# A bidirectional trunk of two layers on Trainium2: scan products that alternate array halves, and dense operands at one place

## The chip, the cores and the metric

One core of one Trainium2 chip runs the whole kernel. Its engines are TensorE (PE, matrix products, with its weight loads PEld), VectorE (DVE), ScalarE (ACT), GpSimd (POOL) and SyncE (SP, which issues transfers). The metric is the device time of one execution in microseconds, less being better.

## The reference

Two layers over 2048 tokens of width 1024, in single precision. The even layer projects the input once; the columns feed a gated DeltaNet (4 heads of 128) and an RWKV-7 time mixing (8 heads of 64), each run forward and backward over the tokens and summed. The odd layer is a Hyena operator with long filters by FFT. After each: an output projection, a LayerNorm, and a gated embedding. What the change touches most is the RWKV-7 recurrence:

```
def step(state, xs):
    r_t, w_t, k_t, v_t, a_t, b_t = xs
    sa = einsum('bhvk,bhk->bhv', state, a_t)
    state = state * w_t[:, :, None, :] + sa[..., None] * b_t[:, :, None, :] + v_t[..., None] * k_t[:, :, None, :]
    return state, einsum('bhvk,bhk->bhv', state, r_t)
...
wkv = rwkv7_scan(r, w_f, k, v, a_vec, b_vec) + flip_t(rwkv7_scan(flip_t(r), flip_t(w_b), ...))
...
h = layer_norm(DEEPNORM_ALPHA * h + mix @ w_out[i], ln_g[i], ln_b[i])
e = rms_norm(p[i] @ ple_w[i], ple_norm[i])
h = h + sigmoid(h @ ple_gate[i]) * e
```

## The kernel before, in words

Seven stages follow one another: the even layer's projection (`phase_a`, 0 to 929 us of the profiled execution), the scans (`scans`, 929 to 2114), a tail (`tail`, output projection, norm and gate, 2114 to 2520), the odd layer's projection (`phase_d`, 2520 to 3330), the Hyena convolutions (3330 to 4120) and the second tail (4120 to 4578).

The dense products (projections and tails) split each single-precision operand into a high and a low part of a faster format and add three products, high with high, low with high and high with low, each 128x128 by 512 columns (for some 80). The moving operands are xh and xl in `phase_a`, hh and hl in `phase_d`; the weights there are wh and wl. In a tail the weights are wo (output projection, in pool tl_o), wg (gate, 8 pairs of tiles in pool tl_w) and we (embedding, 2 pairs, tl_w), printed as tg<-wo0h,yh and so on. Pools place tiles one behind the other in a partition, so the size of one tile sets where the later ones start.

The scans work in chunks of 64 tokens, 32 chunks a direction, first forward, then backward. DeltaNet and RWKV-7 run side by side. RWKV-7 has three parts for a chunk. `rk_front` builds from decay, r, k, a and b the operands X, bk and LY (X and LY have four buffers, `ahead` is 4); for two chunks at once it first forms the decay from w2 and tw (64 rows each, at the upper or lower half of the partitions by direction). Its products ga and gb take the two halves of the rows, four pairs of heads each. An `inverter` then forms the inverse E of a triangular matrix in half precision. `rk_chain` is the recurrence: z from X and the state rS, u from E and z, the new state from bkT and rU, and the outputs y from X with rS and from LY with rU. Products of the recurrence write 64 columns of outputs at one half of the array (a matrix of 64 in its columns: shape 128*64), those of ga and gb use half of its rows (64*128), those of y with X use a quarter (64*64). The chunk's y lies on 64 partitions; ScalarE copies it (forward) or DVE adds it (backward) into Y. `rk_front` for chunk i waits until chunk i − 4 is through the chain (`st["n"]`).

Nothing of the scans is issued as it is written. The class `Ahead` records all engine operations (a call at line 162 runs or records one), and `flush` plans them for all engines at once: `graph` gives each a cost, `forward` walks in time and takes for each free engine the ready operation of the highest priority, `backward` forms new priorities from the plan, up to eleven plans are made, and the shortest by these costs is issued, all at line 638. So all rows of the scans carry L638, and tiles of SBUF are printed as grain.N (pieces of 8 KB that several tiles share) and PSUM tiles as bank. Operations that write one PSUM tile share the highest priority among them (`together`). For PE `forward` prefers, among operations whose priority is within 3.0 us of the best, one of the same `kind` as the last; the kind is a boolean, `slow`: a single-precision product at the lower half of the outputs with over 64 stationary columns.

Of the kernel before, what the change touches and what calls it, by code (L numbers as in the profile page):

```python
# [20 lines left out]
P = 128  # L21
# [122 lines left out]
class Ahead:  # L144
# [101 lines left out]
    class Banks:  # L246
# [7 lines left out]
        def tile(self, shape, dt, name=None, tag=None, bufs=1):  # L254
# [5 lines left out]
            m.bank[name] = base + len(ring) % bufs  # L260
            ring.append(name)
            return m.view(self.t[0][:shape[0], :math.prod(shape[1:])], shape, name)

    def __init__(self, tc):
# [3 lines left out]
        self.plan, self.bank, self.before, self.count, self.exact = None, {}, {}, 0, False  # L268
# [127 lines left out]
    def graph(self, ops):  # L396
# [38 lines left out]
        for i, (e, (w, r)) in enumerate(zip(g["eng"], rw)):  # L435
            if e == "P":
                m = math.prod(r[0].shape[1:])
                g["load"][i] = m / (2400 if ops[i][1] == "transpose" else 1200) if r[-1].dtype == F32 and not self.beside(w[0]) else 0.0
                g["move"][i] = math.prod(w[0].shape[1:]) / (1200 if r[-1].dtype == F32 else 2400)
        g["outer"] = {y: set().union(*(deps[i] for i in users[y])) - users[y] for y in users if y in self.bank}  # L440
# [37 lines left out]
    def together(self, prio):  # L478

        top = {}  # L480
        for y, p in zip(self.g["gen"], prio):
            if y:
                top[y] = max(top.get(y, 0.0), p)
        return [top[y] if y else p for y, p in zip(self.g["gen"], prio)]

    def forward(self, deps, prio, bank=None):
# [16 lines left out]
        order, tick, seen, warm, kind, kept = [], 0, 0.0, False, False, 0.0  # L503
        slow, load, move = g["slow"], g["load"], g["move"]
        while len(order) < n:
# [50 lines left out]
            if e == "P":  # L556
# [5 lines left out]
                seen += cols[i]  # L562
                c = (c + max(0.0, load[i] - kept)) * (1 if warm else 2)
# [37 lines left out]
    def flush(self, stay):  # L601


        self.stay = stay
# [39 lines left out]
class Trunk:  # L644
# [121 lines left out]
    def phase_a(self, src):  # L766
# [3 lines left out]
        with ExitStack() as ctx:  # L770
# [9 lines left out]
            sab = wp.tile([16, 3], F32, name="abs", tag="abs", bufs=1)  # L780
# [465 lines left out]
    @staticmethod  # L1246
    def stages():

        return {"f": {}, "i": {}, "n": 0}
# [160 lines left out]
    def rk_setup(self, d):  # L1410
# [3 lines left out]
        R["w2"] = cp.tile([P, 512], F32, name="rk_w2s")  # L1414
        nc.sync.dma_start(R["w2"][64 * di:64 * di + 64], A["rk_w2"][0, di])
# [12 lines left out]
    def rk_front(self, d, wp, ps, I, st):  # L1428
# [7 lines left out]
        dr = slice(64 * di, 64 * di + 64)  # L1436
        bank = lambda: ps.tile([P, 4, P], F32, name=self.n("pp"), tag="prep", bufs=4)
# [3 lines left out]
        for n, t in enumerate(order(NT)):  # L1441
# [3 lines left out]
            nc.sync.dma_start(tw[dr], self.s_wd[dr, t * P:(t + 1) * P])  # L1445
            while 2 * n >= st["n"] + I["ahead"]:
                yield None
            yield tw,
            p_ = bank()
            for p in range(4):  # L1450
                nc.tensor.matmul(p_[:, p, :], R["w2"][dr, p * P:(p + 1) * P], tw[dr], start=True, stop=True)
# [15 lines left out]
            for j, c in enumerate(order(2)):  # L1467
                i = 2 * n + j
                while i >= st["n"] + I["ahead"]:
# [10 lines left out]
                ga, gb = bank(), bank()  # L1480
                for p in range(4):
                    nc.tensor.matmul(ga[:, p, :], bk[lo, p].rearrange("p q t -> p (q t)"), X[lo, p, 0:2, :], start=True, stop=True)
                for p in range(4):
# [20 lines left out]
    def rk_chain(self, d, wp, ps, st, done, gone):  # L1504
# [4 lines left out]
        bank = lambda: ps.tile([P, 4, 64], F32, name=self.n("ch"), tag="ch", bufs=4)  # L1509
# [752 lines left out]
```

## Time and profile before

| what | value |
|---|---|
| runs, us | 4584.09, 4582.79, 4581.69; median 4582.79 |
| profiled execution, us | 4579.95, its span 4578.0 |
| PE busy, us | 4403.1 (96%) |
| PE weight loads, us | 3674.2 (80%) |
| DVE busy, us | 2798.2 (61%) |
| ACT busy, us | 2325.1 (51%) |
| POOL busy, us | 1741.6 (38%) |
| mean granted clock of PE | 0.982 |

An engine's busy time is the union of its instructions' records. Records of products overlap, since the next starts before the last is drained; what one product costs PE is read from the distance between starts. A single-precision product of the scans leaves two records, others one.

### The profile page before, as it was taken

Reading aid. Unit: us, or ns where it says so; the run is one execution under the profiler, and the core shown is the slowest. Engines: PE = TensorE matmul, PEld = TensorE weight load, DVE = VectorE, ACT = ScalarE, POOL = GpSimd, SP = SyncE. Lnnn points to the kernel's source line nnn. Section 1 sums busy time; section 2 is a strip of 40 time slices with the busy share of each in tenths; the row PEclk is TensorE's granted clock in tenths of the full one; section 3 lists DMA queues with packets and bytes.
Section 4 is the critical chain, followed back from the end, with each engine's and each line's share of the span. In section 5 each row is a group of like instructions: output and inputs, shape, how many; then the busy total and the mean of one; then the engine's idle time right before and its main releaser. Section 6 shows DMA issues by size and latency. Waiting matters only on the chain. (4 is left out here: it accounts for less than half of the span.)

```text
span 4578.0 us, 86860 instructions
## 1 busy us (share of the span) xinstructions
PE 4403.1 (96%) x34638; PEld 3674.2 (80%) x34638; DVE 2798.2 (61%) x4535; ACT 2325.1 (51%) x4533; POOL 1741.6 (38%) x1609
## 2 busy tenths in 40 slices
PE   8999999989999999997999999999989999997999
PEld 6777777778888888885888777777879999986887
DVE  5455555577777788886444334444368888875443
ACT  5334333367667666664222323333279998973222
POOL 0121220244554667764333100000068787763332
PEclk9999999989999999998999999999999999998999
DMA  3233323343333334434211311111131111104211
GB/s 117 71 84 88 86 74 83 88 138 97 105 97 109 120 121 140 139 104 165 68 65 59 102 66 64 64 53 64 51 104 42 50 60 33 48 29 173 71 65 43
DMA packets 379293, 388.95 MB, mean 85 GB/s; under 512 B 111706, under 2 KB 298817, under 8 KB 370441
## 3 DMA queue, kind: packets, MB, share of 16 engines
q1 hardware_dynamic: 378889, 383.40, 26.7%
q8 instruction: 274, 4.49, 0.4%
q14 instruction: 130, 1.06, 0.1%
HBM read 263.18 MB, written 120.13 MB: 84 GB/s over the span
## 5 line engine op out<-in xcount | busy, mean ns | idle before, releaser
L162 ACT COPY pb<-g 128x512 f32<-128x512 f32 (+1 forms) x264 | 154.9, 587 | 900.2 <-PE g L162 900.0
L162 PE MATMUL g<-xh,wh 128*128 128x512 f32 (+1 forms) x1088 | 439.8, 404 | 0.1
L162 PE MATMUL g<-xh,wl 128*128 128x512 f32 (+1 forms) x1088 | 435.1, 400 | 0.0
L162 PE MATMUL g<-xl,wh 128*128 128x512 f32 (+1 forms) x1088 | 434.3, 400 | 0.0
L162 PE MATMUL g<-hh,wh 128*128 128x512 f32 x1024 | 411.2, 402 | 0.5 <-ACT hh L162 0.4
L162 PE MATMUL g<-hl,wh 128*128 128x512 f32 x1024 | 404.3, 395 | 0.0
L162 PE MATMUL g<-hh,wl 128*128 128x512 f32 x1024 | 402.2, 393 | 0.0
L162 DVE SCALAR_TENSOR_TENSOR cv<-pb,pc,cv 128x512 f32<-128x512 f32 (+1 forms) x304 | 225.7, 749 | 181.9 <-ACT pb L162 95.8
L638 POOL MEMSET grain.4123_32497<- 64x2048 f32 x1 | 1.8, 1801 | 756.5 <-PE g L162 756.5
L162 PEld LDWEIGHTS g<-xh,wh 128*128 128x128 f32 (+1 forms) x1088 | 206.3, 190 | 52.8 <-issue 3.7
L162 PEld LDWEIGHTS g<-xl,wh 128*128 128x128 f32 (+1 forms) x1088 | 205.7, 189 | 50.8 <-DVE xl L162 0.4
L162 PEld LDWEIGHTS g<-xh,wl 128*128 128x128 f32 (+1 forms) x1088 | 206.1, 189 | 49.1 <-issue 0.7
L162 POOL TENSOR_TENSOR sq<-tm 128x512 f32<-128x512 f32 x48 | 51.9, 1092 | 481.2 <-ACT tm L162 481.2
L162 PEld LDWEIGHTS g<-hh,wh 128*128 128x128 f32 x1024 | 192.3, 188 | 50.3 <-ACT pb L162 3.2
L162 PEld LDWEIGHTS g<-hl,wh 128*128 128x128 f32 x1024 | 192.3, 188 | 48.9
L162 PEld LDWEIGHTS g<-hh,wl 128*128 128x128 f32 x1024 | 192.3, 188 | 47.5 <-issue 1.9
L162 ACT CAST h<-sp 128x512 fp32r<-128x512 f32 (+1 forms) x96 | 46.2, 513 | 336.5 <-PE sp L162 336.5
L162 DVE SCALAR_TENSOR_TENSOR u<-u,tg 128x512 f32<-128x512 f32 x64 | 44.0, 687 | 239.8 <-PE tg L162 239.8
L162 POOL TENSOR_TENSOR yl<-y,yh 128x1024 fp32r<-128x1024 f32 x32 | 78.1, 2440 | 283.8 <-ACT yh L162 283.8
L162 DVE SCALAR_TENSOR_TENSOR pm<-pb,hcol,a 128x512 f32<-128x512 f32 x64 | 73.2, 1155 | 148.6 <-ACT pb L162 148.1
L162 DVE SCALAR_TENSOR_TENSOR a<-pb,hcol,a 128x512 f32<-128x512 f32 x128 | 94.4, 741 | 104.7 <-ACT pb L162 65.5
L162 ACT ACTIVATE tg<-tg 128x512 f32<-128x512 f32 x64 | 37.2, 582 | 214.7 <-PE tg L162 214.7
(733 smaller groups left out, 13286.9 us busy)
## 6 DMA issues: line engine op xcount, KB each, us to landing
grain.45_7042<-s_rk SPq DMA_DIRECT2D x32, 1024.0 KB
wr<-in_even_w_in SPq DMA_DIRECT2D x33, 512.0 KB
y<-s_y SPq DMA_DIRECT2D x32, 512.0 KB
wr<-in_odd_w_in SPq DMA_DIRECT2D x32, 512.0 KB
xr<-in_x SPq DMA_DIRECT2D x32, 256.0 KB
s_qk<-cm SPq DMA_DIRECT2D x32, 256.0 KB
s_kv<-tm SPq DMA_DIRECT2D x32, 256.0 KB
s_gate<-th SPq DMA_DIRECT2D x32, 256.0 KB
```

Of the source, the lines that this page charges most:

```text
L162: f(*a, **kw)
L638: r = f(*map(bare, a), **{k: bare(x) for k, x in kw.items()})
```

## The change

Two things change. The first is in the scans. `flush` gets a flag that only the scans set: a product's kind is then which of the four array shapes it uses, a change of kind costs 0.095 in the plan, a product on a part of the array costs half as much as before unless it sits in the same place as the one before it, and weight loads cost nothing. Two PSUM tiles can be twins that share a priority. ga and gb are twins and are written alternately. The outputs y of two chunks are formed together when the second is through, in twin tiles, with products that alternate over the array, and are copied or added on 128 partitions; rS and rU get a third buffer for that, and `rk_front` waits for a count `st["m"]` that rises by two when a pair's y is written. w2 is filled up with zeros to 128 rows, and tw is loaded with all 128 rows. The second is in the dense stages: a tile is widened and two unused ones are put in front, so that later tiles start elsewhere. In bytes mod 512 of a partition, moving and stationary operand go from 224 and 256 to 224 and 224 in `phase_a`, from 64 and 224 to 224 and 224 in `phase_d`, from 160 and 224 to 224 and 224 for wg, and from 160 and 32 to 224 and 32 for we; for wo they are 224 and 224 before and after.

```diff
@@ -251,13 +251,15 @@
-        def tile(self, shape, dt, name=None, tag=None, bufs=1):
+        def tile(self, shape, dt, name=None, tag=None, bufs=1, twin=None):
...
             m.bank[name] = base + len(ring) % bufs
+            m.twin[name] = m.twin[twin.name] if twin is not None else name
             ring.append(name)
@@ -265,7 +267,7 @@
-        self.plan, self.bank, self.before, self.count, self.exact = None, {}, {}, 0, False
+        self.plan, self.bank, self.twin, self.before, self.count, self.exact = None, {}, {}, {}, 0, False
@@ -437,6 +439,18 @@
+        g["part"], g["spot"] = [None] * len(ops), [0] * len(ops)
+        if self.parts:
+            for i, (e, (w, r)) in enumerate(zip(g["eng"], rw)):
+                if e == "P":
+                    k, m = r[0].shape[0], math.prod(r[0].shape[1:])
+                    g["part"][i] = (k > 64, m > 64)
+                    where = lambda x: x.offset // x.ap[0][0] % P >= 64
+                    g["spot"][i] = where(w[0]) + 2 * where(r[0])
+                    if g["part"][i] != (True, True) and r[-1].dtype == F32:
+                        g["cost"][i] = 0.004 + max(math.prod(w[0].shape[1:]), 52) / 1200, g["cost"][i][1]
+                    g["load"][i], g["slow"][i] = 0.0, g["part"][i]
         g["outer"] = {y: set().union(*(deps[i] for i in users[y])) - users[y] for y in users if y in self.bank}
@@ -478,10 +492,11 @@
         top = {}
-        for y, p in zip(self.g["gen"], prio):
+        gen = [y and self.twin[y] for y in self.g["gen"]]
+        for y, p in zip(gen, prio):
             if y:
                 top[y] = max(top.get(y, 0.0), p)
-        return [top[y] if y else p for y, p in zip(self.g["gen"], prio)]
+        return [top[y] if y else p for y, p in zip(gen, prio)]
@@ -500,7 +515,7 @@
         got, spare, rows = {}, [(0.0, k) for k in range(8)], []
-        order, tick, seen, warm, kind, kept = [], 0, 0.0, False, False, 0.0
+        order, tick, seen, warm, kind, kept, spot, parts = [], 0, 0.0, False, False, 0.0, 0, self.parts
@@ -560,6 +575,13 @@
                 seen += cols[i]
+                if parts:
+                    if kind != slow[i]:
+                        c += 0.095
+                    elif slow[i] != (True, True) and spot == g["spot"][i]:
+                        c *= 2
+                    spot = g["spot"][i]
                 c = (c + max(0.0, load[i] - kept)) * (1 if warm else 2)
@@ -598,10 +620,11 @@
-    def flush(self, stay):
-        self.stay = stay
+    def flush(self, stay, parts=False):
+        self.stay, self.parts = stay, parts
         ops, self.plan, self.exact = self.plan, None, True
@@ -777,7 +800,7 @@
             rk = wp.tile([P, T], F32, name="rk", tag="rk", bufs=1)
-            sab = wp.tile([16, 3], F32, name="abs", tag="abs", bufs=1)
+            sab = wp.tile([16, 128], F32, name="abs", tag="abs", bufs=1)[:, 0:3]
@@ -1246,7 +1269,7 @@
-        return {"f": {}, "i": {}, "n": 0}
+        return {"f": {}, "i": {}, "n": 0, "m": 0}
@@ -1412,6 +1435,7 @@
         R["w2"] = cp.tile([P, 512], F32, name="rk_w2s")
+        nc.gpsimd.memset(R["w2"][64 - 64 * di:P - 64 * di], 0.0)
         nc.sync.dma_start(R["w2"][64 * di:64 * di + 64], A["rk_w2"][0, di])
@@ -1433,8 +1457,7 @@
         lo, hi, al = slice(0, 64), slice(64, 128), slice(0, P)
-        dr = slice(64 * di, 64 * di + 64)
-        bank = lambda: ps.tile([P, 4, P], F32, name=self.n("pp"), tag="prep", bufs=4)
+        bank = lambda twin=None: ps.tile([P, 4, P], F32, name=self.n("pp"), tag="prep", bufs=4, twin=twin)
@@ -1442,13 +1465,13 @@
             tw = sb("tw", [P], 2)
-            nc.sync.dma_start(tw[dr], self.s_wd[dr, t * P:(t + 1) * P])
-            while 2 * n >= st["n"] + I["ahead"]:
+            nc.sync.dma_start(tw, self.s_wd[:, t * P:(t + 1) * P])
+            while 2 * n >= st["m"] + I["ahead"]:
                 yield None
...
             for p in range(4):
-                nc.tensor.matmul(p_[:, p, :], R["w2"][dr, p * P:(p + 1) * P], tw[dr], start=True, stop=True)
+                nc.tensor.matmul(p_[:, p, :], R["w2"][:, p * P:(p + 1) * P], tw, start=True, stop=True)
             G = sb("G", [4, P], 1)
@@ -1466,7 +1489,7 @@
                 i = 2 * n + j
-                while i >= st["n"] + I["ahead"]:
+                while i >= st["m"] + I["ahead"]:
                     yield None
@@ -1477,10 +1500,10 @@
                 yield bk, X
-                ga, gb = bank(), bank()
+                ga = bank()
+                gb = bank(ga)
                 for p in range(4):
                     nc.tensor.matmul(ga[:, p, :], bk[lo, p].rearrange("p q t -> p (q t)"), X[lo, p, 0:2, :], start=True, stop=True)
-                for p in range(4):
                     nc.tensor.matmul(gb[:, p, :], bk[hi, p].rearrange("p q t -> p (q t)"), X[hi, p, 1:3, :], start=True, stop=True)
@@ -1506,7 +1529,7 @@
         NC = 2 * NT
-        bank = lambda: ps.tile([P, 4, 64], F32, name=self.n("ch"), tag="ch", bufs=4)
+        bank = lambda twin=None: ps.tile([P, 4, 64], F32, name=self.n("ch"), tag="ch", bufs=4, twin=twin)
@@ -1514,7 +1537,7 @@
             for nm in ("rS", "rU"):
-                x = sb(nm, [4, 2, 64], 2)
+                x = sb(nm, [4, 2, 64], 3)
                 v = self.s_rv[tok(i):tok(i) + 64].rearrange("t s (a c) -> t s a c", a=4)
@@ -1524,7 +1547,7 @@
         nc.vector.memset(rS[hi, :, 1, :], 0.0)
-        Y = None
+        Y, two = None, []
         for i in range(NC):
@@ -1538,7 +1561,7 @@
             t, c, X, LY, E, bkT, pcl = (u[k] for k in ("t", "c", "X", "LY", "E", "bkT", "pcl"))
-            hp = slice(64 * c, 64 * c + 64)
+            two.append((slice(64 * c, 64 * c + 64), X, LY, rS, rU))
             if i + 1 < NC:
@@ -1566,23 +1589,31 @@
                 nc.vector.tensor_tensor(nS[hi, :, 1, :], pd[hi], sp[hi], op=ALU.add)
-            py = [bank(), bank()]
-            for p in range(4):
-                for q, r in ((0, lo), (1, hi)):
-                    nc.tensor.matmul(py[q][hp, p, :], X[r, p, 1, :], rS[r, p, q, :], start=(p == 0), stop=False)
-            for p in range(4):
+            if i % 2:
+                py = [bank()]
+                py.append(bank(py[0]))
+                for p in range(4):
+                    for k in range(2):
+                        for j, (hp, X, _, S_, _) in enumerate(two):
+                            q = k ^ j
+                            r = (lo, hi)[q]
+                            nc.tensor.matmul(py[q][hp, p, :], X[r, p, 1, :], S_[r, p, q, :], start=(p == 0), stop=False)
+                for p in range(4):
+                    for q in range(2):
+                        for hp, _, LY, _, U_ in two:
+                            nc.tensor.matmul(py[q][hp, p, :], LY[:, p, q, :], U_[:, p, q, :], start=False, stop=(p == 3))
                 for q in range(2):
-                    nc.tensor.matmul(py[q][hp, p, :], LY[:, p, q, :], rU[:, p, q, :], start=False, stop=(p == 3))
-            for q in range(2):
-                if late:
-                    nc.vector.tensor_tensor(Y[hp, :, q, :], py[q][hp], Y[hp, :, q, :], op=ALU.add)
-                else:
-                    nc.scalar.copy(Y[hp, :, q, :], py[q][hp])
-            if i % 2:
+                    if late:
+                        nc.vector.tensor_tensor(Y[:, :, q, :], py[q], Y[:, :, q, :], op=ALU.add)
+                    else:
+                        nc.scalar.copy(Y[:, :, q, :], py[q])
+                two = []
                 if late:
...
                     nc.sync.dma_start(self.s_ro[t], Y.rearrange("p a s c -> p (a s c)"))
+                st["m"] += 2
             if i + 1 < NC:
@@ -1651,7 +1682,7 @@
                 self.weave(ch + iv + fr + po)
-            nc.flush(3.0)
+            nc.flush(3.0, True)
@@ -1763,6 +1794,7 @@
+            wp.tile([P, 16], F32, name=f"off{i}")
             wo, we, wg = weights(op, f"wo{i}", KT), weights(wp, f"we{i}", 2), weights(wp, f"wg{i}", KT)
@@ -1822,6 +1854,7 @@
             xp = ctx.enter_context(tc.tile_pool(name="pd_x", bufs=1, reuse_waits="tile"))
+            xp.tile([P, 40], F32, name="off")
             xh = xp.tile([P, KT, T], F32R, name="hh")
```

The first place is on PE in the forward scan's first chunk, before the change: z's eight products, from X (grain.55) and the state (grain.38) on 64 of the 128 outputs, printed 64x64.

```order
L638 MATMUL bank3_7028<-grain.1_7033,grain.104_7049 128x128
L638 MATMUL bank0_7025<-grain.38_7040,grain.55_7044 64x64 x6
L638 LDWEIGHTS grain.55_7044
L638 MATMUL bank1_7026<-grain.60_7045,grain.55_7044 128x64
...
L638 MATMUL bank0_7025<-grain.38_7040,grain.55_7044 64x64
L638 MATMUL bank5_7030<-ident_60,grain.55_7044 128x128 x4
...
L638 MATMUL bank6_7031<-grain.29_7039,grain.60_7045 128x64
L638 MATMUL bank0_7025<-grain.38_7040,grain.55_7044 64x64
L638 MATMUL bank2_7027<-grain.38_7040,grain.1_7033 128x128
```

The same products after the change, on PE, with the products ga and gb (bk in grain.83 and X) ahead of them.

```order
L661 MATMUL bank3_7028<-grain.83_7048,grain.55_7044 128x128
L661 MATMUL bank7_7032<-grain.83_7048,grain.55_7044 128x128 x4
L661 MATMUL bank3_7028<-grain.83_7048,grain.55_7044 128x128 x3
L661 LDWEIGHTS grain.55_7044
L661 MATMUL bank2_7027<-grain.60_7045,grain.55_7044 128x64
...
L661 MATMUL bank1_7026<-grain.38_7040,grain.55_7044 64x64 x8
L661 LDWEIGHTS grain.60_7045
L661 MATMUL bank0_7025<-grain.83_7048,grain.60_7045 128x64
```

z's products stood in three places, six, one and one, with half-precision products (those with a LDWEIGHTS of their own) and whole ones between; now they stand in one run of eight.

The second place is on PE at the first outputs y, before the change: products of one chunk in bank1, with half-precision products of the inverse in bank7 between.

```order
L638 MATMUL bank6_7031<-grain.15_7038,grain.104_7049 128x64
L638 MATMUL bank1_7026<-grain.38_7040,grain.55_7044 64x64 x3
L638 LDWEIGHTS grain.15_7038
L638 MATMUL bank7_7032<-grain.83_7048,grain.15_7038 128x64
...
L638 MATMUL bank7_7032<-grain.15_7038,grain.83_7048 128x64
L638 MATMUL bank1_7026<-grain.38_7040,grain.55_7044 64x64
L638 LDWEIGHTS grain.60_7045
L638 MATMUL bank4_7029<-grain.104_7049,grain.60_7045 128x64
```

After the change: the products of two chunks, from grain.38 and grain.55 and from grain.157 and grain.83, in the twins bank6 and bank2.

```order
L661 MATMUL bank3_7028<-grain.213_7055,grain.73_7046 128x128 x2
L661 MATMUL bank6_7031<-grain.38_7040,grain.55_7044 64x64
L661 MATMUL bank6_7031<-grain.157_7051,grain.83_7048 64x64
...
L661 MATMUL bank2_7027<-grain.157_7051,grain.83_7048 64x64
L661 MATMUL bank2_7027<-grain.38_7040,grain.55_7044 64x64
...
L661 MATMUL bank6_7031<-grain.157_7051,grain.83_7048 64x64
L661 LDWEIGHTS grain.15_7038
L661 MATMUL bank4_7029<-grain.169_7052,grain.15_7038 128x64
```

Sixteen products of a pair of chunks stand together and alternate between the chunks, where those of one chunk stood in several places.

## Rows read from the trace of the kernel before

**Rows 1.** Windows by stage: stretch, length, busy us and count by engine, PE clock, DMA.

```profile
0.00:929.00 929.00, 886.12 (x3986) 700.45 (x3986) 500.48 (x785) 362.70 (x598) 160.66 (x132) 0.98 0.31 87
929.00:1500.00 571.00, 557.61 (x7937) 478.44 (x7938) 429.96 (x894) 391.92 (x887) 283.16 (x305) 0.98 0.35 107
1500.00:2114.00 614.00, 589.79 (x8510) 504.31 (x8508) 515.38 (x1084) 411.07 (x936) 413.14 (x412) 1.00 0.40 121
```

**Rows 2.** Timeline of PE, dense products: start, length, engine, line, operation; pairs 24 products apart.

```profile
2213.18 0.39 PE L162 MATMUL tg<-wo0h,yh 128*128 128x512 f32 x1
2218.62 0.39 PE L162 MATMUL tg<-wo0h,yh 128*128 128x512 f32 x1
...
520.11 0.40 PE L162 MATMUL g<-xh,wh 128*128 128x512 f32 x1
525.71 0.40 PE L162 MATMUL g<-xh,wh 128*128 128x512 f32 x1
...
2990.63 0.40 PE L162 MATMUL g<-hh,wh 128*128 128x512 f32 x1
2996.23 0.40 PE L162 MATMUL g<-hh,wh 128*128 128x512 f32 x1
...
2199.91 0.40 PE L162 MATMUL tg<-wg0h,h 128*128 128x512 f32 x1
2205.52 0.39 PE L162 MATMUL tg<-wg0h,h 128*128 128x512 f32 x1
```

**Rows 3.** Timeline of PE, scans; x counts records, two a single-precision product (transposes one).

```profile
1172.29 0.28 PE L638 MATMUL bank<-grain.15_7038,grain.83_7048 128*128 128x64 f16 x4
1172.41 1.14 PE L638 MATMUL bank<-grain.203_7054,grain.73_7046 128*128 128x128 f32 x8
1173.38 0.60 PE L638 MATMUL bank<-ident,grain.55_7044 128*128 128x128 f32 x4
...
1003.27 0.29 PE L638 MATMUL bank<-grain.169_7052,grain.134_7050 128*128 128x64 f16 x4
1003.49 0.68 PE L638 MATMUL bank<-grain.157_7051,grain.83_7048 128*64 128x64 f32 x8
1004.10 0.40 PE L638 MATMUL bank<-grain.1_7033,grain.301_7057 128*128 128x128 f16 x4
...
983.39 0.34 PE L638 MATMUL bank<-grain.38_7040,grain.77_7047 128*64 128x64 f32 x4
983.66 0.30 PE L638 MATMUL bank<-grain.169_7052,grain.9_7037 128*128 128x64 f16 x4
...
1310.07 0.69 PE L638 MATMUL bank<-grain.157_7051 128*64 128x64 f32 x16
1310.69 0.40 PE L638 MATMUL bank<-grain.104_7049,grain.222_7055 128*128 128x128 f16 x4
...
1154.07 1.06 PE L638 MATMUL bank<-grain.203_7054,grain.77_7047 128*128 128x128 f32 x8
1154.96 0.28 PE L638 MATMUL bank<-grain.203_7054,grain.15_7038 128*128 128x64 f16 x4
```

**Rows 4.** Lines of DVE from 1500 to 2114: a group's busy time, mean ns, idle before.

```profile
L638 DVE TENSOR_TENSOR grain.38_7040<-bank,grain.38_7040 64x256 f32<-64x256 f32 x32 | 13.1, 418 | 4.0 <-PE bank L638 1.9 <-ACT grain.55_7044 L638 1.8
```

**Rows 5.** Waits from 1000 to 2105: who, for whom, us in total, times, longest.

```profile
POOL grain.55_7044 L638 <- PE bank L638: 91.2, 49, 8.2
```

**Rows 6.** Timeline of PE and DVE: inverses' first uses, chunks 0, 16 and 63, and their fronts.

```profile
978.99 0.34 PE L638 MATMUL bank<-grain.157_7051 128*64 128x64 f32 x4
...
1220.12 0.61 DVE L638 TENSOR_TENSOR grain.55_7044<-grain.45_7042,grain.55_7044 128x256 f32<-128x256 f32 x1
1270.98 0.68 PE L638 MATMUL bank<-grain.157_7051,grain.203_7054 128*64 128x64 f32 x14
...
2072.41 0.41 DVE L638 TENSOR_TENSOR grain.55_7044<-grain.45_7042,grain.55_7044 128x256 f32<-128x256 f32 x1
2103.22 0.69 PE L638 MATMUL bank<-grain.157_7051,grain.203_7054 128*64 128x64 f32 x16
```

## The prediction

> **What bounds the kernel now.** The page comes first: TensorE (PE) is busy 4403.1 of 4578.0 us, 96%, VectorE (DVE) 61%, ScalarE 51%, GpSimd (POOL) 38%. One engine that is nearly always busy ends the kernel, so the question is what its busy time consists of. The second view is the windows by stage [rows 1]: PE is busy 95% of the first projection, 557.6 of 571 us in the first half of the scans and 589.8 of 614 in the second. Beside it DVE is busy 75% in the first half and 84% in the second, where more has to be post-processed, and PE's idle share goes from 2.3% to 3.9%. So PE bounds both stages that the change touches, and in the scans DVE stands next. The third view is PE's own timeline, since a busy PE need not run at its best: there the distance from the start of one product to the start of the next is its price, which the busy time alone hides (the modelled ends overlap the next start).
>
> **The change, its dense part.** The four dense groups are the same product, 128x128 by 512 columns, and differ in where moving and stationary operand start in a partition: the same place mod 512 bytes for wo, different places for the first projection, the second one and the tails' gate wg. In [rows 2], 24 of wo's start within 5.44 us, 0.2267 each; 24 of the first projection's, of the second's and of wg's within 5.60, 5.60 and 5.61, 0.2335 each. wg's and wo's stretches lie 13 us apart in one stage, so the stage doesn't explain it; what else differs is that wo's weights lie in another pool. The shift makes the three slow groups like wo in this respect and touches 3264 products of the first projection, 3072 of the second, 1536 of wg: 7872. By [rows 2] that is 7872 x 0.0067 = 52 us. The mean over all neighbours less than 0.26 apart is 0.2274 against 0.2333, which gives 47; with the longer distances in, waits and all, 0.2357 against 0.2404, 37. I take −47, the middle one, since it has most products behind it and no waits in it. The hyena stage and the small product we keep different places: 0.
>
> In [rows 2] the product is slower where its weights come from another place. [...]
>
> **The scans: shape changes.** PE's array is used whole (128*128) or in halves (128*64 and 64*128) or quarters. The prices are read in [rows 3]. A run of half-precision products of four costs 0.12 when the next product has the same shape (1172.29 to 1172.41), 0.22 when the shape changes (1003.27 to 1003.49): +0.10 on entering. Two products that alternate between the halves and what follows cost 0.27 (983.39 to 983.66), eight 0.62 (1310.07 to 1310.69): 0.058 each and 0.154 left over per visit, for leaving. So a visit costs 0.25, a change of shape 0.125. Four products on one half take 0.61 (1003.49 to 1004.10), 0.114 each without the 0.154: not alternating costs 0.0565 more. Whole single-precision products cost 0.2225 among themselves (four in 0.89, 1154.07 to 1154.96), and four that begin behind a half-precision product 0.97 (1172.41 to 1173.38): +0.08.
>
> Counted in the written order of the two programs, 12,494 products in the scans: shape changes go from 1613 to 746, 867 x 0.125 = −108. Neighbours on the same half, among the 128*64 and 64*64 ones, go from 653 to 92, 561 x 0.0565 = −32. Those of shape 64*128 go from 391 to 241; their price has no unbroken row here, so I bound it by nothing and by the whole product's 0.22 and take half of it, as for the columns: 150 x 0.11 = −17. Against that, whole single-precision products right behind a half-precision one go from 79 to 438, 359 x 0.08 = +29. The 128 products with w2 move from a half array to a whole one, 0.22 there against at most the same before: 0. Sum −128. Priced another way, each product by the median distance of its own kind with its own two neighbours' kinds over the whole trace, the scans' products come to 1131 us before (PE's busy time there is 1147 [rows 1]) and 965 after, −166. The two differ in products beside a change that the few rows don't show; I take the middle, −147.
>
> **What else the scans get.** Y's sums run on 128 partitions instead of 64: in the backward scan 64 instructions of 0.418 (32 of them in [rows 4]) become 32 of the same length, 13 us off DVE and as much off ScalarE in the forward one. PE bounds, so that counts only through the next paragraph. The double tw transfers and two memsets of zeros lie beside PE work, 16 small transfers a scan: 0; uncovered, a memset would cost about 2 once.
>
> **What is late next.** With 147 gone in proportion, the halves last about 498 and 541 if PE's idle stays as it is, while DVE's work stays 430 and falls to 502: 86% and 93% busy. The first half then stands where the second does now, 3.9% idle, some +6. For the second, where the idle share nearly doubled between 75% and 84%, I double it and a little more, 24 to 54, +30. Together +36; between +25 (idle share of the second half hardly rising) and +46. Scans net −147 + 36 = −111.
>
> **Sum.** −111 − 47 = −158 on the profiled execution's 4579.95 us gives 4422; the median of the runs stands 2.8 above that execution, so 4425. Range: −166 − 52 + 0 would be 4365 as the low end; 4510 from −38 in the scans and −37 dense (below), with 2.5 to spare.
>
> **Rivals.**
> *PE gets all of it.* What the other engines wait for is mostly PE, as X's writer does [rows 5], and the give-back stays out: 4580 − 147 − 47 = 4386, to 4365 with −166. For it: the waits on PE end as PE speeds up. Against: idle rose with DVE's share.
>
> *The loop of four bounds.* The front of a chunk may start only when X and LY of the chunk four earlier are free: those 91.2 us in 49 waits are GpSimd's, which writes X. The recurrence's steps are (2103.22 − 978.99)/63 = 17.85 apart [rows 6], four are 71.4, of which 57 go from a front's first product on DVE to the use of its inverse (mean over 64 chunks; 50.9 from 1220.12 to 1270.98, and 30.8 in the last, 2072.41 to 2103.22, where PE has little else), and 14 are the end of the chain. Now two chunks' Y are formed together and both are given back with the second, some 7 later. A loop is then latency + 21. If the latency falls only to 48, with PE's queue shorter but not short, a step is 69/4 = 17.25, 63 x 0.6 = −38 in the scans, and 4580 − 38 − 47 + 3 = 4498. For it: PE's own work per step falls by 147/63 = 2.3 while the loop has grown by 7. Against: 30.8 unloaded leaves much room, and the latency is mostly queueing on PE.
>
> *The places don't matter.* If the 3% comes from its pool or its use, the dense term is 0: 4425 + 47 = 4472. [...] Against: three groups in three stages, all at 0.2335.
>
> *Slower, the same loop.* The first chunk of a pair can't free its X and LY until the second is through. On POOL, SP and DVE the front's instructions of the next pair stand behind that, on POOL the scaled states sp too, which the chain itself needs. If the latency stays 57, a step is 78/4 = 19.5, 63 x 1.65 = +104, less 47: 4580 + 57 + 3 = 4640. It outweighs the dense gain from a latency of 53.4 up (step 18.6). For it: 91.2 us of waits at just that place. Against: PE must then be idle some 290 us in the scans, with all else equal, and queueing shrinks when it is.
>
> **How the numbers follow.** Forecast, 4395 to 4455 as its own range: 0.50. PE gets all: 0.17. Loop of four: 0.18. Places don't matter: 0.08. Slower by the loop: 0.05. What is left, 0.02, is about no change. What a measurement here can tell from no change is about 0.2%, 9 us. So faster 0.93, same 0.02, slower 0.05. The range from 4365 to 4510 takes in the forecast and the first three rivals but for their tails, and leaves out about 0.15.
>
> **What would show it.** Dense: 24 products of g with xh and hh, and of tg with wg, start within 5.45 instead of 5.60. Scans: runs of eight products of 128*64 within 0.62, four-product runs of half precision seldom at 0.22; the stage 1185 long before, 1075 after. Give-back: PE's idle time in the scans near 74 instead of 38, with DVE at 86 to 93%. Steps near 16.1; if they are above 17 with PE idle over 100 us and POOL's waits for PE at X well above 91, the loop bounds. It is wrong if the products of the scans don't come nearer to one another, or if dense distances stay at 0.2335.

## The result, and the profile after

The changed kernel takes 4407.88 us (median of 4 runs, 4402.19 to 4412.97), before 4583.44 in the same comparison: ratio 0.9616, interval 0.9600 to 0.9633, 176 us faster. The forecast was 4425, its own range 4395 to 4455. The profiled execution took 4402.19 us, its span 4400.3.

The two profiled executions differ by 178 us. Counted from the first product of a stage to the first of the next (the last stage to its last product), that is:

| stage | before, us | after, us | difference | forecast |
|---|---|---|---|---|
| first projection | 924.8 | 908.0 | −16.8 | |
| scans | 1200.1 | 1069.3 | −130.9 | −111 |
| first tail | 438.8 | 434.1 | −4.7 | |
| second projection | 764.3 | 745.3 | −19.0 | |
| Hyena | 807.4 | 806.1 | −1.3 | 0 |
| second tail | 431.4 | 426.5 | −4.9 | |
| dense stages together | | | −45.4 | −47 |

The windows by stage of the changed kernel (first projection, forward scan, backward scan; columns as in [rows 1], the last ones PE's clock, DMA share and GB/s):

```profile
0.00:912.00 912.00, 865.11 (x3986) 696.78 (x3986) 500.45 (x785) 362.59 (x598) 161.20 (x133) 0.98 0.34 89
912.00:1432.00 520.00, 495.25 (x8310) 436.25 (x8311) 447.91 (x942) 391.48 (x897) 297.21 (x323) 0.98 0.43 129
1432.00:1966.00 534.00, 494.87 (x8135) 434.18 (x8134) 485.84 (x1004) 390.49 (x894) 403.16 (x396) 0.99 0.42 130
```

In the two windows of the scans PE is busy 990.1 us, 157 less than the 1147.4 of [rows 1], and idle 63.9, 26 more than 37.6. DVE is busy 86% and 91% of them.

The dense products on the changed kernel's PE timeline, pairs 24 apart, against [rows 2]:

```profile
518.97 0.39 PE L162 MATMUL g<-xh,wh 128*128 128x512 f32 x1
524.41 0.39 PE L162 MATMUL g<-xh,wh 128*128 128x512 f32 x1
...
2800.01 0.39 PE L162 MATMUL g<-hh,wh 128*128 128x512 f32 x1
2805.45 0.39 PE L162 MATMUL g<-hh,wh 128*128 128x512 f32 x1
```

Both take 5.44 us where they took 5.60; 5.44 is what wo took before.

How the products of one step were scattered in the kernel before can be read from its PE timeline, at the first chunk's eight products with the inverse (shape 128*64, two records each):

```profile
978.99 0.34 PE L638 MATMUL bank<-grain.157_7051 128*64 128x64 f32 x4
979.25 0.23 PE L638 MATMUL bank<-grain.15_7038,grain.104_7049 128*128 128x64 f16 x2
979.42 0.45 PE L638 MATMUL bank<-grain.157_7051 128*64 128x64 f32 x6
979.79 0.29 PE L638 MATMUL bank<-grain.104_7049,grain.29_7039 128*128 128x64 f16 x4
979.92 0.28 PE L638 MATMUL bank<-grain.29_7039,grain.104_7049 128*128 128x64 f16 x4
980.13 0.45 PE L638 MATMUL bank<-grain.157_7051 128*64 128x64 f32 x6
980.51 0.40 PE L638 MATMUL bank<-grain.1_7033,grain.169_7052 128*128 128x128 f16 x4
```

The same eight on the changed kernel's PE timeline:

```profile
962.46 0.28 PE L661 MATMUL bank<-grain.169_7052,grain.134_7050 128*128 128x64 f16 x4
962.66 0.69 PE L661 MATMUL bank<-grain.157_7051 128*64 128x64 f32 x16
963.28 0.29 PE L661 MATMUL bank<-grain.104_7049,grain.15_7038 128*128 128x64 f16 x4
...
1955.77 0.69 PE L661 MATMUL bank<-grain.157_7051,grain.201_7054 128*64 128x64 f32 x16 [0.43 <-DVE grain.201_7054 L661]
```

Before, the eight products came in three visits of two, three and three that took 0.26, 0.37 and 0.38 us, 1.01 in all; in one visit they take 0.62. The last line is the last use of an inverse. From the first to the last there are 63 steps of the recurrence, so a step is (1955.77 − 962.66)/63 = 15.76 us long, against 17.85 before.

What waits for what in the changed kernel's scans, us in total, times, longest (X's writer from 983 to 1957; then the longest sum among PE's waits from 912 to 1966):

```profile
POOL grain.55_7044 L661 <- PE bank L661: 68.5, 38, 6.7
...
PE bank L661 <- DVE grain.15_7038 L661: 14.2, 25, 1.8
```

GpSimd's wait at X fell from 91.2 [rows 5] to 68.5; PE's waits for DVE, all lines of the view together, rose from 14.6 us in 39 waits to 38.6 in 73.

### The profile page after: what moved, and what is told of

Its sections match the earlier page's. It is cut to its first block, busy times and chain, and to the rows that moved or that the text cites. A ratio compares the mean times of both kernels' runs of the same rounds, so it can differ in the third digit from the quotient of the medians.

```text
span 4400.3 us, 86695 instructions
## 1 busy us (share of the span) xinstructions
PE 4194.5 (95%) x34638; PEld 3555.3 (81%) x34638; DVE 2785.8 (63%) x4503; ACT 2303.9 (52%) x4501; POOL 1745.8 (40%) x1611
## 4 chain that ended last, share of the span: by engine, by line
PE 45%; ACT 4%; POOL 2%; issue 1%; DVE 1%; DMA 1%; SPq 0%; POOLq 0%; ACTq 0%; DVEq 0%
PE tg L162 17%; PE g L162 16%; PE bank L661 11%; PE sp L162 1%; POOL grain.4098_32449 L661 0%; ACT grain.4035_32414 L661 0%; POOL grain.4090_32447 L661 0%; PE tr L162 0%; ACT grain.4036_32415 L661 0%; ACT grain.4039_32418 L661 0%; ACT grain.4037_32416 L661 0%; POOL grain.4200_32456 L661 0%; POOL grain.4186_32455 L661 0%; DMA e<-in_w_out 0%; ACT grain.4045_32424 L661 0%
```

## The experiments

For the scans I priced an order by giving each product the median distance that its kind and neighbours have in the trace before. "Waits" are what is left of the scans' time, from their first product to their last, when this price is taken off; a granted clock of PE below 1 (0.97 to 0.99 over the windows of the scans) and short pauses are among them. "PE idle" is read from windows. "Scans" run from their first product to the tail's first.

| kernel | shape changes | priced | waits | PE idle | PE waits for DVE | scans | median |
|---|---|---|---|---|---|---|---|
| before | 1612 | 1131 | 53 | 38 | 14.6 | 1200 | 4583 |
| changed | 745 | 965 | 87 | 64 | 38.6 | 1069 | 4408 |
| planner_only | 842 | 1030 | 111 | 67 | 40.4 | 1156 | 4534 |
| no_planner | 1513 | 1067 | 61 | 44 | 22.1 | 1144 | 4483 |
| no_pairs | 774 | 1013 | 91 | 60 | 36.6 | 1120 | 4456 |
| dve_less | 785 | 973 | 84 | 62 | 29.8 | 1072 | 4406 |
| dve_more | 738 | 971 | 108 | 73 | 48.4 | 1095 | 4428 |
| five_xl | 747 | 964 | 92 | 64 | 37.4 | 1072 | 4407 |
| stay_1 | 962 | 1007 | 55 | 44 | 22.1 | 1079 | 4415 |
| stay_5 | 659 | 951 | 111 | 78 | 48.8 | 1078 | 4414 |

(planner_only has the dense places of before, the others those of the change.)

**The two halves apart.** place_only adds to the kernel before the three edits of tiles; scans_only takes them out of the changed one.

```diff
-            sab = wp.tile([16, 3], F32, name="abs", tag="abs", bufs=1)
+            sab = wp.tile([16, 128], F32, name="abs", tag="abs", bufs=1)[:, 0:3]
...
+            wp.tile([P, 16], F32, name=f"off{i}")
...
+            xp.tile([P, 40], F32, name="off")
```

> The kernel before, with only the tiles of the dense stages moved, so that moving and stationary operand start at one place mod 512 bytes. Theory (place decides): from the first product of one stage to that of the next, the first projection falls by 17 us, the second by 19, the tails by 5 each, as in the changed kernel, the scans stay at 1200; 4583 - 46 = 4537 us, and all three dense groups start 0.2272 apart. Rival (the shorter dense stages come with the other half of the change, for instance through transfers that start earlier): 4583, distances stay at 0.2333.

> The changed kernel with the dense tiles put back where they were. Theory (two parts that only add): the scans last 1069 us from their first product to the tail's first, 131 less than before, dense distances are 0.2333 again; 4583 - 131 = 4452 us. Rival (the parts help each other, the place also speeds the scans): above 4460 and the scans above 1075.

place_only: 4542.34 against 4581.44, ratio 0.9914 (0.9899 to 0.9929), −39, 5 us above the theory's 4537. The dense stages give −39 (first projection −11, second −18, tails −5 each), the scans +4. scans_only: 4453.83, ratio 0.9723 (0.9707 to 0.9739), −128, its scans 1072.6. The two ratios multiply to 0.9639, the change has 0.9616: within their intervals the halves only add. The first projection's gain was 11 to 17 us over the runs that have the new place, so the dense term is 39 to 46, and the 47 of the prediction stands just above that.

**Which places are alike.** Two probes shift single groups. The diff is the first one; the second has 32 columns for sab, 48 and 32 for off, 112 and 16 around wo, and 72 for off_w.

```diff
-            sab = wp.tile([16, 128], F32, name="abs", tag="abs", bufs=1)[:, 0:3]
+            sab = wp.tile([16, 64], F32, name="abs", tag="abs", bufs=1)[:, 0:3]
...
-            wp.tile([P, 16], F32, name=f"off{i}")
+            wp.tile([P, (24, 80)[i]], F32, name=f"off{i}")
+            if i == 0:
+                op.tile([P, 16], F32, name="off_o")
             wo, we, wg = weights(op, f"wo{i}", KT), weights(wp, f"we{i}", 2), weights(wp, f"wg{i}", KT)
+            if i == 0:
+                op.tile([P, 112], F32, name="off_p")
...
+            wp.tile([P, 88], F32, name="off_w")
             xp.tile([P, 40], F32, name="off")
```

> The changed kernel with five dense groups put at chosen places (moving, stationary, bytes mod 512): first projection 224 and 480, second 64 and 64, wo of the first tail 288 and 224, wg of the first tail 256 and 224, wg of the second 480 and 224; wo of the second tail stays at 224 and 224. Theory (equal mod 512 is what counts): only the second projection and the second tail's wo keep 0.2270 between starts, the others stand at 0.233. Rival one (equal mod 256 is enough): the first projection and the second tail's wg keep 0.2270 too. Rival two (the place 224 itself counts): the second projection goes to 0.233. Rival three (wo is faster by its pool or its use): the first tail's wo keeps 0.2270. By the theory the time is 17 + 5 + 5 + 5 us above the changed kernel's, about 4440.

> The changed kernel with other places for the dense groups (moving, stationary, bytes mod 512): first projection 224 and 352, second 0 and 0, wo of the first tail 160 and 224, wg of the first tail 352 and 224, wg of the second 288 and 224; wo of the second tail stays at 224 and 224. Open after the first probe: whether equal mod 128 is enough too, and why 64 apart gave 0.2289 for wo. Theory (equal mod 256 is needed): the first projection and the first tail's wg, 128 apart, go to 0.233, the second projection stays at 0.2270, the tails' groups 64 apart stand at 0.229 or 0.233 by which operand is ahead. Rival (mod 128 is enough): the first projection and the first tail's wg keep 0.2270.

The first probe's PE timeline, pairs 24 apart: first projection (256 bytes apart), wo of the first tail (64), wg of the first tail (32):

```profile
518.74 0.39 PE L162 MATMUL g<-xh,wh 128*128 128x512 f32 x1
524.18 0.39 PE L162 MATMUL g<-xh,wh 128*128 128x512 f32 x1
...
2077.42 0.39 PE L162 MATMUL tg<-wo0h,yh 128*128 128x512 f32 x1
2082.91 0.39 PE L162 MATMUL tg<-wo0h,yh 128*128 128x512 f32 x1
...
2147.94 0.39 PE L162 MATMUL tg<-wg0h,h 128*128 128x512 f32 x1
2153.54 0.39 PE L162 MATMUL tg<-wg0h,h 128*128 128x512 f32 x1
```

The second probe's first projection, 128 bytes apart, and wo, 64 apart the other way:

```profile
519.06 0.40 PE L162 MATMUL g<-xh,wh 128*128 128x512 f32 x1
524.64 0.39 PE L162 MATMUL g<-xh,wh 128*128 128x512 f32 x1
...
2082.40 0.39 PE L162 MATMUL tg<-wo0h,yh 128*128 128x512 f32 x1
2087.99 0.40 PE L162 MATMUL tg<-wo0h,yh 128*128 128x512 f32 x1
```

Means of the distances below 0.26 us between starts, by how many bytes the moving operand's place lies above the stationary one's:

| difference, bytes | mean distance, us |
|---|---|
| 0 (both at 224, at 64 or at 0) | 0.2270 |
| 256 either way | 0.2271 and 0.2275 |
| +64 | 0.2289 (wo) and 0.2289 (wg) |
| −64 | 0.2333 |
| +32 | 0.2334 |
| +128 and −128 | 0.2328 and 0.2326 |

So for the projections, wo and wg the place 224 and the pool don't matter; equal mod 256 is enough (0.2271 and 0.2275 at 256 apart), which the first expectation had as its rival; mod 128 is not (0.2328 and 0.2326 at 128 apart). The tails' small we, 256 apart in the second probe's second tail, is less clear: 85 of its 156 distances are at most 0.228, but the mean is 0.2293. In time, one run each, 4421.95 and 4432.51 us: the first stays below its 4440 because the first projection and the second wg kept their pace. Why the moving operand 64 bytes ahead costs only a third of what the other offsets cost (0.0019 against 0.0056 to 0.0064 above 0.2270) stays open.

**Planner and pairs apart.** planner_only adds to the kernel before the new kind and prices alone; no_planner takes them out of the changed kernel; no_pairs forms each chunk's y by itself, with two buffers for rS and rU and a count per chunk.

```diff
-            nc.flush(3.0, True)
+            nc.flush(3.0)                                      # no_planner
...
-            if i % 2:
-                py = [bank()]
+            py = [bank(), bank()]                              # no_pairs, as before
```

> The kernel before with the planner's part of the change alone: the kind by array shape, the price of a change, the price of the same place; no twins, no outputs by pairs, dense tiles as before. Shape changes of its order are 842 (before 1612, changed kernel 745), neighbours on the same half 771 (653, 92). Theory (each product's price is set by its own kind and its neighbours'): priced by the median distances of the kernel before, the scans' products cost 1030 us instead of 1131, some 20 us come back as waits, so the scans last about 1120 and the kernel 4503. Rival (the outputs by pairs are what helps, since they save instructions and weight loads, the grouping only moves waits): scans above 1170, kernel above 4550.

> The changed kernel with the planner's new kind and prices switched off; twins, outputs by pairs and dense places stay. Its order has 1513 shape changes (before 1612, changed kernel 745), 50 same-half neighbours. Theory (products are priced by kind and neighbours): 1067 us of products instead of 965, 64 less than before; waits at least the 53 of before, so the scans last about 1125 to 1140 and the kernel 4465 to 4480. Rival (outputs by pairs gain by themselves, by fewer copies and sums and by freeing DVE, whatever the order): scans below 1100, kernel below 4440.

> The changed kernel with each chunk's outputs formed by themselves again (and one count for the front); planner, twins of ga and gb, and dense places stay. Shape changes 774, same-half neighbours 746. Theory: products priced at 1013 us, 48 above the changed kernel's; with its waits of 87 to 110 the scans last 1115 to 1140, the kernel 4455 to 4480. Rival (pairing costs the front its early release, so that without it waits go back to 53): scans about 1083, kernel about 4422.

Windows of the scans, first planner_only:

```profile
927.00:2068.00 1141.00, 1073.85 (x16440) 943.22 (x16440) 952.66 (x1977) 798.11 (x1822) 698.89 (x717) 0.97 0.38 119
```

no_planner:

```profile
917.00:2046.00 1129.00, 1084.55 (x16444) 932.52 (x16444) 928.59 (x1945) 788.29 (x1791) 694.78 (x718) 0.99 0.39 121
```

no_pairs:

```profile
913.00:2018.00 1105.00, 1044.66 (x16441) 921.86 (x16441) 942.97 (x1977) 798.25 (x1822) 697.93 (x718) 0.98 0.40 124
```

no_planner and no_pairs came out as the theory had them, 1144 (a little above its 1140) and 1120. planner_only fell between theory and rival: products priced at 1030 as said, but waits of 111, not some 75. PE stood idle hardly more than in the changed kernel (67 against 64); most of what its waits have over the changed kernel's 87 is PE's clock, 0.97 here against 0.99. Windows of planner_only at the change of direction show it:

```profile
1490.00:1495.00 5.00, 3.30 (x49) 2.48 (x46) 2.15 (x4) 4.43 (x14) 3.50 (x4) 1.00 0.68 241
1495.00:1500.00 5.00, 3.83 (x34) 3.01 (x32) 4.91 (x6) 4.29 (x11) 3.54 (x3) 0.56 0.19 68
1500.00:1515.00 15.00, 13.68 (x128) 11.41 (x129) 10.33 (x22) 6.67 (x13) 9.20 (x10) 0.50 0.01 3
1515.00:1520.00 5.00, 5.00 (x90) 4.65 (x89) 3.48 (x9) 4.09 (x11) 0.40 (x1) 0.89 0.64 211
```

After five us in which PE was busy 3.30, at a granted clock of 1.00, the clock was 0.56 for five us, 0.50 for 15 and 0.89 for five; what made it fall is not shown. What such a stretch costs can be read in the changed kernel's first projection: products 128x128 by 512 start 0.427 apart from 466.24 to 468.37 us, at a clock of 0.50, and 0.226 apart from 474.76 to 475.89, at 1.00. Over the scans and the pause behind them, slices of 4 us, each times what its clock lacks to 1, sum to 40 us in planner_only, 20 before, 23 in the changed kernel. So the new kind makes the shape changes go (−770 by itself, −44 us). The pairs make the products alternate: neighbours on the same half are 771 in planner_only, 746 in no_pairs, 92 in the change. Neither the planner alone (−44) nor pairs and twins alone (−56 in no_planner) give half of the 131.

**What is late.** dve_less and dve_more move one multiplication a chunk off DVE or onto it; five_xl gives X and LY a fifth buffer.

```diff
-                nc.vector.tensor_tensor(bk[:, :, 0], x4, en, op=ALU.mult)
+                nc.gpsimd.tensor_tensor(bk[:, :, 0], x4, en, op=ALU.mult)   # dve_less
-                nc.gpsimd.tensor_tensor(bk[:, :, 1], y4, en, op=ALU.mult)
+                nc.vector.tensor_tensor(bk[:, :, 1], y4, en, op=ALU.mult)   # dve_more
-                X, bk, LY = sb("X", [4, 3, 64], I["ahead"]), sb("bk", [4, 2, 64], 1), sb("LY", [4, 2, 64], I["ahead"])
+                X, bk, LY = sb("X", [4, 3, 64], I["ahead"] + 1), sb("bk", [4, 2, 64], 1), sb("LY", [4, 2, 64], I["ahead"] + 1)   # five_xl
```

> The changed kernel with one multiplication per chunk (x by the decay, 64 in all, 0.4 to 0.6 us each on DVE) moved from DVE to GpSimd; priced order 973 us instead of 965. Theory (DVE at 89% is what is late behind PE): DVE's busy time in the scans falls from 934 to about 900, PE's waits for DVE from 38.6 to under 28, the scans by some 8 after the 8 of the order, kernel about 4400 to 4408. Rival (the grouping of kinds itself delays urgent products, and PE then waits for whatever stood behind them, whoever is busy): PE's waits for DVE stay at 35 to 45, kernel 4415 or more, GpSimd's longer work only adding to it.

> The changed kernel with one multiplication per chunk (y by the decay, 64 in all) moved from GpSimd to DVE, the reverse of an earlier run: DVE's busy time in the scans rises from 934 to about 968, products priced at 971 us instead of 965. Theory (the grouping makes most of the waits, DVE's load a smaller part): as the reverse took 9 us off PE's waits for DVE, these rise from 38.6 to some 48, scans about 1084, kernel about 4422. Rival (DVE's load makes all of the waits): at 91% they rise by 20 or more, kernel 4434 or more.

> The changed kernel with five buffers for X and LY instead of four (priced order 964 us, as the changed kernel's 965). Theory (the loop of four doesn't bind, DVE is late): GpSimd's waits for PE at X fall from 68.5 to under 40, the scans stay within 8 us of 1069, kernel 4400 to 4416. Rival (the loop of four, lengthened by the pairs, is where the give-back comes from): PE's idle time falls from 64 towards 38, the scans last 1045 or less, kernel 4384 or less.

Windows of the scans, dve_less:

```profile
911.00:1969.00 1058.00, 996.32 (x16444) 873.89 (x16444) 899.84 (x1881) 781.10 (x1790) 742.24 (x782) 0.99 0.42 129
```

dve_more:

```profile
912.00:1992.00 1080.00, 1006.92 (x16443) 882.78 (x16444) 963.60 (x2009) 786.57 (x1790) 651.07 (x654) 0.98 0.41 126
```

five_xl, its waits at X:

```profile
POOL grain.55_7044 L661 <- PE bank L661: 64.5, 43, 5.8
```

dve_less: 34 us less on DVE take 9 off PE's waits for it (29.8, where the theory had under 28), but only 3 off the waits of the table (those for ScalarE and GpSimd rose by 5 together); its time, 4405.91, is in the theory's range and no different from the changed kernel's. dve_more: 30 us more add 10 to PE's waits for DVE and 21 to the waits of the table, and 20 us to the kernel, 6 of them by price; by time it lies between its two expectations (4428.08). So DVE's load matters, upward more than downward, and which share of the waits it makes these two don't settle. five_xl gives 4407.37, ratio 0.9614 (0.9598 to 0.9631), no difference; X's writer waits nearly as long and idle time is 64 as before. The buffer thus failed to shorten the wait that it was meant to, so this run says only that a fifth buffer there gains nothing. no_pairs says more: with each chunk's X and LY given back by itself GpSimd's wait at X is 48.2, 20 less than with pairs, yet PE is idle 60 where the changed kernel has 64. The pairs do hold the front back, and PE doesn't pay for it.

**The grouping itself.** stay_1 and stay_5 change the band within which the planner prefers the present kind.

```diff
-            nc.flush(3.0, True)
+            nc.flush(1.0, True)                                # stay_5: 5.0
```

> The changed kernel with the planner's band for staying with a kind cut from 3.0 us to 1.0: 962 shape changes instead of 745, products priced at 1007 us instead of 965. Theory (the grouping itself makes the waits, since it holds back products that others wait for): PE's waits for DVE fall from 38.6 to 28 or less, products' waits in all from 87 to about 65, scans about 1090, kernel about 4429. Rival (the waits come from DVE's load alone, which is the same work in a longer stage): waits fall by less than 8, scans 1100 or more, kernel above 4440.

> The changed kernel with the band raised from 3.0 us to 5.0: 659 shape changes, products priced at 951 us instead of 965. Theory (the grouping makes the waits): waits rise by as much as the products save or more, scans 1069 to 1085, kernel 4408 to 4424, PE's waits for DVE above 42. Rival (DVE's load alone): waits rise by 5, scans about 1060, kernel about 4399.

Windows of the scans, stay_1:

```profile
917.00:1981.00 1064.00, 1019.66 (x16444) 888.40 (x16444) 927.98 (x1945) 784.93 (x1791) 702.72 (x718) 0.99 0.42 128
```

stay_5:

```profile
915.00:1978.00 1063.00, 984.99 (x16443) 869.24 (x16444) 939.91 (x1945) 782.60 (x1790) 702.64 (x718) 0.98 0.42 128
```

With a band of 1.0 the products cost 42 more by price and the waits are 55, nearly those of before, though DVE does the same work at 87%; with 5.0 the products cost 14 less and the waits are 111. Price and waits change places, and the scans stay within 10 us. Both runs came out on the theory's side, stay_1 beyond it (waits of 55 where it had some 65, 4415 where it had 4429). A least length of the stage, set by the recurrence and not by PE's order, would let price and waits change places in the same way. Against it, no_pairs has the band of the changed kernel and products 48 us dearer, and its waits are 91, not fewer than the 87. The kernels' ratios, 0.9638 (0.9623 to 0.9652) and 0.9637 (0.9621 to 0.9653), overlap with the change's, so by time the three bands are hardly told apart. No variant here beats the changed kernel beyond its interval.

## Why the prediction was right, and where its sum was off

**Direction and bound.** PE bounds the stages (in the changed kernel it is busy 95% of the first projection and 94% of the scans), and the price of a product between its neighbours decides. Shown: the medians of kinds before, put on the nine other orders of the table, come within 2.5% of what each order's own medians give, and what is left is waits of 53 to 111.

**Dense term.** Forecast −47, measured −45 in this trace, −39 with the places alone. That the place decides and not the pool is shown by wo, which went from 0.2270 to 0.2289 and 0.2333 when it was shifted, and by wg, which stood at 0.2289 and 0.2334 when its place was 64 and 32 bytes off. Why the place decides is not shown. The condition was named too narrowly, mod 512 for mod 256.

**Price of the scans.** This is the term that was mis-sized. The sum took −147, the middle between −128 by a few rows and −166 product by product. PE's busy time fell by 157; priced with the medians of before the new order costs 166 less, and with each order's own medians about 180 less. By each of these −147 was too little. Part of what the rows missed can be seen above: the visits in [rows 3] had two and eight products, and an odd number costs as much as the next even one, three 0.377 to 0.384 for four, one 0.261 to 0.267 for two (medians of before). 483 visits to part of the array had an odd number, 137 have now; 346 x 0.05 = 17 of the 38 that part the two sums. The rest isn't told apart.

**What is late next.** The forecast's +36 was of idle time, which rose by 26 (63.9 where it had near 74), at the lower end of its +25 to +46. (In proportion the halves would have been 500 and 538 us long, not 498 and 541; that leaves the +36 as it was.) So by PE's records the 20 us that the scans came out below −111 are shared evenly: 10 more saved in busy time, 10 less given back in idle time. By prices all of the 20 lie in the price, −166 for −147, and the waits rise by 34 (87 − 53); but these waits are what the price leaves over, so their nearness to 36 confirms nothing. The reason given held only in part: the give-back followed from DVE's rising share, and stay_1 has a share of 87% with waits of 55. Most of the waits go with the band: 55, 87 and 111 at 1.0, 3.0 and 5.0, PE's waits for DVE 22.1, 38.6 and 48.8. That the planner then holds back a product that others wait for until its kind has its turn is how I read it, not shown product by product. DVE's load adds to it, as dve_more shows. By DVE's share alone, stay_5 would have gained.

**Rivals.** "PE gets all of it" was too low by 22 (4386, which leaves out the 2.8 between execution and median, 4389 with it): waits did come back. "The loop of four" (4498) and its slower form (4640) are out: a step is 15.76 where the first needed 17.25, GpSimd's wait at X fell, taking the pairs away cut it further but left the waits at 91, and with the pairs kept and a band of 1.0 they are 55. "The places don't matter" is out by place_only (−39 in the dense stages). That the memsets and the doubled tw transfers cost nothing was not tried by itself; the two memsets of w2 took 0.52 us each in the changed kernel's trace, not about 2, and the Hyena stage stayed the same (−1.3).

## What to carry to other kernels

Where PE bounds, price each product by the distance to the next start, by its kind and by the kinds beside it, from the trace, and put these prices on the new order product by product: here that gave −166 where PE's busy time fell by 157, and a few hand-picked rows gave −128. Grouping alike work on the engine that bounds was paid for in waits (87, and 55 and 111 with a shorter and a longer reach); vary how far it may reach before blaming the next busiest engine. Let moving and stationary operand of products like these, 128x128 by 512 columns, start at the same place mod 256 bytes (0.2270 to 0.2275 us a product here, 0.2289 to 0.2334 at the other offsets tried).

## What the runs showed of the hardware

- A 128x128 by 512 product in the faster format starts 0.2270 us after the last with both operands at one place, 0.2271 and 0.2275 with the places 256 bytes apart, 0.2289 with the moving one 64 ahead, 0.2326 to 0.2334 at the other offsets tried (−64, +32, 128 either way, and the −32 and −160 of before).
- Products on half of the array that alternate between output halves start 0.058 apart, on the same half 0.116 (medians of before); an odd one at the end of a run costs as much as two, three 0.377 and four 0.384.
- A whole single-precision product is dearer behind a half-precision one, about 0.30 against 0.223 (medians of before), and the new order has 438 such places where the old one had 79.
- In planner_only PE's granted clock was 1.00 from 1490 to 1495 us, with PE busy 3.30 of the 5, 0.56 from 1495 to 1500, 0.50 from 1500 to 1515 and 0.89 from 1515 to 1520. What its clock lacked to 1 over the scans and the pause behind them sums to 40 us, 20 more than in the kernel before. At a clock of 0.50 a 128x128 by 512 product started 0.427 us after the last, at 1.00 0.226 (changed kernel, first projection).
